# Head scales by transposes of a broadcast column, filling products kept for the end of attention, and four stores moved to ScalarE, in a two-layer hybrid encoder

## The chip, the cores and the metric

The kernel runs on one core of one Trainium2 chip. The metric is device time in microseconds (us) of one launch, which does all of the work from the input arrays in device memory (DRAM) to the two outputs. TensorE does the matrix products and transposes, VectorE, ScalarE and GpSimd the elementwise work, and DMA queues, issued mostly by SyncE, move data between DRAM and the on-chip memories: SBUF, and PSUM, which has eight banks of 128 x 512 float32 and receives the results of TensorE. In the rows of the profile these engines are PE (PEld for its weight loads), DVE, ACT, POOL and SP.

## The reference

Two layers are applied to two sequences with the same weights: a prompt of 2048 rows and a sample of 512 rows, each row 1024 wide.

```python
def layer(x, l, ...):
    h = rms_norm(x, pre_g)
    proj = h @ w_in                                    # 1024 -> 3072
    u, zp, q, k, v, za = split(proj)                   # 512 each
    pool_out = multiscale_pool(u, pool_w, pool_scale) * silu(zp)
    q, k = rope(q), rope(k)                            # 4 heads, 2 maps, 64 wide
    o = diff_attention(q, k, v, lam)                   # softmax(q1 k1) v - lam * softmax(q2 k2) v
    o = rms_norm(o, subln_g, 1e-5) * (1 - lambda_init) # over the 128 of each head
    attn_out = o * silu(za)
    y = concat(pool_out, attn_out) @ w_out             # 1024 -> 1024
    return x + rms_norm(y, post_g)
```

Everything is float32. Attention is bidirectional (no mask), each sequence attends to itself only, and its four heads have values of 128 columns.

## The kernel before, in words

**Number format.** [...] The kernel splits an operand into a high and a low half (`split`: a copy to `F32R`, then a subtraction) and adds the products high x high, low x high and high x low, so one tile of 128 x 128 weights against 512 columns costs three products.

**Order of a layer** (`Layer.run`).

1. *Norm and projections.* Rows are normalised, transposed by TensorE and split (`hth`, `htl`), 512 rows at a time. `project` makes 128 x 512 blocks of `proj` in the four PSUM banks named `sc`, each with 24 products. `evacuate` takes such a block out of PSUM and stores it to DRAM: q and k with their rotation (`qs`, `ks`), v (`vs`), the pool inputs (`us`, `zs`), and the gate za as `(tanh(za/2) + 1) * za` in `gs`, one store for each of four heads and each 512 rows. All these stores are issued on SyncE.

2. *Attention* (`attention`). One block is 256 queries of one head; the prompt's last head alternates with the sample's blocks. The work runs in steps. A step of the steady state issues, in this order: four pairs of score products (`score`, L439 and L440, q high and q low against 512 keys) mixed with the four exponentials of the previous step's scores (`expo`, L466) and the maxima of this step (`peak`); one flip after the first pair and one after the last (`flip`, L491: four transposes of the exponentials into a `tr` bank, of which there are two; `split` then makes `ath` on ScalarE and `atl` on VectorE); the values products of the earlier step's late flip; the combination of the two softmax maps on GpSimd (`combine`, L481 and L482); filling products; and the values products of the early flip. `values` (L508) accumulates a block's output in the one PSUM bank `ot`. A prompt block takes four steps, and its values take eight flips.

When a block's last values are out, `finish` (L512 to L526) runs as a generator over the step: ScalarE copies `ot` to `oc`; between the early and the late flip's split VectorE makes `mt` = oc times a column `sg` times the gate `g`, which goes to DRAM (`mh`); after the late split ScalarE squares `oc` and copies the high half, and VectorE subtracts for the low half (`shl`). One step later `squares` multiplies these with a matrix of ones (L532), and `scales` takes from it the head's RMS scale for each query, `rstat`, 128 queries on the partitions and one column per head.

At the end of attention some steps have no scores: only flips, values and what is left of the finishing remain. I call them end steps.

3. *Filling products* (`fill`, called at L653). While attention runs, `fill(n)` issues up to n products of other work into the one PSUM bank `mm`: first the sample's projections to q, k, v and za (16 groups of 24 products, of which the first four steps take two groups, L277; for v, L249, `fill` counts two products of half the columns as one), then, after the second half of the weights `w_out` is loaded and split (steps without products), the pooled half of the output projection (`pooled_outputs`, 20 tiles of two groups of 12 products, L697), whose results go to DRAM (`ys`). Each group ends by yielding its evacuation, and there the loop of `fill` breaks, so that a call never passes the end of a group. n is 14 in steps 0 to 3 (`FIRST`) and 6 from then on (`FILL`). The evacuation begins in the next step. What is left after attention is issued in a row by a loop in `Layer.run`, which in this kernel finds nothing.

4. *Phase 3* (`phase3`). For each of 20 tiles of 128 rows (16 of the prompt, 4 of the sample), `load` fetches the pooled half `y` and `mixh` (the `mt` of four heads), and prepares `diag` on GpSimd: `rstat`'s four columns are split into a high and a low half (`r2`) and multiplied into identity matrices (L764). `scale` multiplies ones with the eight diagonals, two products into a `tr` bank (L771), so that each head's scale stands on every partition, 128 queries along the columns. VectorE multiplies the bank with `mixh` to `mixs`, and splits it to `hl`: the high half is copied on ScalarE, the low half subtracted on VectorE. `products` issues 24 products (L784) into two `sc` banks, VectorE adds `y`; `post` squares on ScalarE, scales on VectorE, adds the residual `xr` on GpSimd (L834) and stores. `scale` for tile n + 1 runs beside the products of tile n. In layer 0 the last tiles also carry the norm of the next layer's first rows (`prepare`).

**Who sets the order.** On TensorE, ScalarE, VectorE and GpSimd instructions run in the order in which the program issues them. On SyncE a planner places them; it issues in order, and a store whose data is late holds back those behind it. Buffers in SBUF come in pools with a fixed number of turns (`bufs`), and `reuse_waits="tile"` makes the next user of a buffer wait for the last reader.

Of the kernel before, what the change touches and what calls it, by code (L numbers as in the profile page):

```python
# [15 lines left out]
ALU = mybir.AluOpType  # L16
# [25 lines left out]
FIRST = 14  # L42
WGAP = 3
# [7 lines left out]
def f32(ap):  # L51
    return ap.bitcast(F32)
# [3 lines left out]
def trunk_kernel(ctx: ExitStack, tc: tile.TileContext, a, outs):  # L56
# [227 lines left out]
    def evacuate(st, sl, kind, pair, sub, ps, cs, raws, p):  # L284
# [7 lines left out]
        if kind in ("za", "zp"):  # L292
            th = p["t"].tile([P, TB], F32, name="rb")
            nc.scalar.activation(th, ps, AF.Tanh, scale=0.5)
            o = p["t"].tile([P, TB], F32, name="ra")
            nc.scalar.activation(o, ps, AF.Copy)
            yield
            nc.vector.scalar_tensor_tensor(o, th, 1.0, o, op0=ALU.add, op1=ALU.mult)
            nc.sync.dma_start(st["gs" if kind == "za" else "zs"][h][:, sl], o)
            return  # L300
# [92 lines left out]
    def attention(c, p, po, fill):  # L393
# [118 lines left out]
        def finish(b):  # L512
            st, h, qb, ot = b["st"], b["h"], b["qb"], b["ot"]
            qs = slice(qb * QB, (qb + 1) * QB)
            oc = p["o"].tile([P, QB], F32, name="oc")
            nc.scalar.activation(oc, ot[:, :QB], AF.Copy)  # L516
            yield
            mt = p["o"].tile([P, QB], F32, name="mt")
            nc.vector.scalar_tensor_tensor(mt, oc, c["sg"], b["g"], op0=ALU.mult, op1=ALU.mult)
            nc.sync.dma_start(st["mh"][:, h, qs], mt)  # L520
            yield
            shl = p["o"].tile([P, 2, QB], F32R, name="shl", bufs=2)
            nc.scalar.activation(oc, oc, AF.Square)
            nc.scalar.activation(shl[:, 0], oc, AF.Copy)
            nc.vector.tensor_tensor(shl[:, 1], oc, f32(shl[:, 0]), op=ALU.subtract)  # L525
            closing.append((b, oc, shl))  # L526
# [63 lines left out]
        while True:  # L590
# [62 lines left out]
            fill(FILL if step > 3 else FIRST)  # L653
# [84 lines left out]
    def phase3(l, wo, scaling, pairs, kept, es, nxt):  # L738
# [4 lines left out]
        m_p = mixed.enter_context(sbuf("m", 2))  # L743
# [5 lines left out]
        def load(st, t):  # L749

            s = dict(st=st, t=t, y=y_p.tile([P, D], F32, name="y"))
            nc.sync.dma_start(s["y"], st["ys"][t * P : (t + 1) * P, :])
            t0 = t // 2 * 2 * P
            key = st["n"], t0
            if key not in pairs:
                pairs[key] = d_p.tile([P, H, 2 * P], F32, name="mixh")
                nc.sync.dma_start(pairs[key], st["mh"][:, :, t0 : t0 + 2 * P])
            s["h"] = pairs[key][:, :, t % 2 * P : (t % 2 + 1) * P]
            r = st["rstat"][:, t, :]
            r2 = small.tile([P, 2, H], F32R, name="r2")  # L760
            split(r2[:, 0], r2[:, 1], r, nc.gpsimd, nc.gpsimd)
            s["diag"] = d_p.tile([P, 2 * H, P], F32R, name="diag")
            wide = f32(r2).rearrange("p i h -> p (i h)").unsqueeze(2).to_broadcast([P, 2 * H, P])
            nc.gpsimd.tensor_tensor(s["diag"], ident.unsqueeze(1).to_broadcast([P, 2 * H, P]), wide, op=ALU.mult)  # L764
            tiles.append(s)

        def scale(s):

            ps = bank("tr")
            for i in range(2):  # L770
                nc.tensor.matmul(ps, lhsT=ones, rhs=s["diag"][:, i * H : (i + 1) * H, :].rearrange("p h n -> p (h n)"), start=i == 0, stop=i == 1)  # L771
# [4 lines left out]
            split(s["hl"][:, 0], s["hl"][:, 1], m, nc.scalar, nc.vector)  # L776
# [66 lines left out]
        for _ in scale(tiles[0]):  # L843
            pass
        scaling = []
        for n in range(len(order)):
# [5 lines left out]
            if n + 1 < len(order):  # L852
                scaling.append(scale(tiles[n + 1]))
# [316 lines left out]
```

## Time and profile before

| | before |
|---|---|
| median of 3 runs | 3190.98 us (3190.53 to 3191.36) |
| profiled execution | 3190.91 us |
| its span, first to last instruction | 3189.1 us |
| TensorE busy (PE) | 3086.4 us, 97% |
| VectorE (DVE) | 2187.3 us, 69% |
| GpSimd (POOL) | 1859.2 us, 58% |
| ScalarE (ACT) | 1749.7 us, 55% |
| mean granted TensorE clock | 0.992 |
| DMA | 464.54 MB, mean 146 GB/s |

The times in the traces are counted from the span's start. A row of a group of instructions names its line, engine and operation, the tiles it writes and reads, the shape and the count, then the busy time and the mean duration of one, then the idle time in front and what ended it. A row of the timeline has the start, the duration, the engine, and the line, with the wait before it in square brackets. A row of a window has its bounds and length, then the busy time of PE, PEld, DVE, ACT and POOL with the number of their instructions (of PE and PEld alone where one line was asked for), then the granted clock, the busy share of the DMA engines and GB/s.

Attention runs from 630.89 to 1432.20 in layer 0 and from 2217.54 to 3015.93 in layer 1, each time up to the first end step. Phase 3 of layer 1 begins at 3045.21.

### The profile page before, as it was taken

To read this page: it belongs to the slowest core of one execution; us is meant where nothing else is said; L and a number is where in the kernel's file an instruction comes from. 1 tells how busy PE (TensorE), PEld (TensorE's weight loads), DVE (VectorE), ACT (ScalarE), POOL (GpSimd) and SP (SyncE) were. 2 spreads that over 40 slices of the span, in tenths; PEclk is the share of its full clock that TensorE was granted. 3 is DMA by queue.
4 is the path that set the end of the run, shared out by engine and by line. 5 is a ranking of instruction groups with operands and counts; after the bars stand their busy time and mean duration, and the time that the engine had idled before them with its cause. 6 is when DMAs were issued, how large, how long until landed. Compare 5 with 4: busy or idle time off the path is not lost. (4 is left out here: it accounts for less than half of the span.)

```text
span 3189.1 us, 48499 instructions
## 1 busy us (share of the span) xinstructions
PE 3086.4 (97%) x16936; PEld 2590.8 (81%) x16936; DVE 2187.3 (69%) x3289; ACT 1749.7 (55%) x3995; POOL 1859.2 (58%) x2058
## 2 busy tenths in 40 slices
PE   8999999999998999998899999999999999999988
PEld 6898888778887888887688888887788878888866
DVE  3354255678898887777834543555888988877777
ACT  3244233377777777772333432333787778777622
POOL 1000122289997988888810001222999979888888
PEclk9999999999999999999999999999999999999999
DMA  5354457643424334437754544577434253353367
GB/s 203 113 160 144 129 160 208 196 132 96 130 67 129 107 109 138 120 99 242 269 176 123 160 131 142 164 204 213 115 90 123 63 141 111 95 156 110 107 213 239
DMA packets 298901, 464.54 MB, mean 146 GB/s; under 512 B 26144, under 2 KB 180768, under 8 KB 298656
## 3 DMA queue, kind: packets, MB, share of 16 engines
q1 hardware_dynamic: 298656, 461.44, 48.4%
q8 instruction: 133, 2.18, 0.3%
q14 instruction: 112, 0.92, 0.1%
HBM read 293.57 MB, written 167.77 MB: 145 GB/s over the span
## 5 line engine op out<-in xcount | busy, mean ns | idle before, releaser
L466 ACT ACTIVATE e<-sc,nm 128x512 f32<-128x512 f32 x1088 | 733.3, 694 | 49.2 <-DVE nm L453 39.7
L450 DVE TENSOR_REDUCE mx<-sc 128x1 f32<-128x512 f32 x1024 | 648.1, 682 | 143.5 <-PE sc L440 141.9
L482 POOL TENSOR_TENSOR e<-e,e 128x1024 f32<-128x1024 f32 (+1 forms) x288 | 666.4, 2314 | 24.0
L277 PE MATMUL sc<-hth,wh 128*128 128x512 f32 x1408 | 555.4, 394 | 0.1
L277 PE MATMUL sc<-htl,wh 128*128 128x512 f32 x1408 | 554.1, 394 | 0.2 <-DVE htl L114 0.2
L277 PE MATMUL sc<-hth,wl 128*128 128x512 f32 x1408 | 552.4, 392 | 0.0
L439 PE MATMUL sc<-ks,q 128*128 128x512 f32 x1024 | 435.6, 425 | 11.8 <-DMA ks<-ks_p 5.3
L109 ACT ACTIVATE ath<-tr 128x512 fp32r<-128x512 f32 x544 | 327.9, 606 | 215.6 <-PE ot L508 167.6
L440 PE MATMUL sc<-ks,q 128*128 128x512 f32 x1024 | 405.5, 396 | 0.0
L114 DVE TENSOR_TENSOR atl<-tr,ath 128x512 fp32r<-128x512 f32 x544 | 364.0, 682 | 43.5 <-ACT ath L109 43.5
L508 PE MATMUL ot<-ath,v 128*128 128x256 f32 x2176 | 369.3, 292 | 3.1 <-ACT oc L516 1.9
L491 PE MATMUL tr<-ident,e 128*128 128x128 f32 x2176 | 330.6, 275 | 18.0 <-DVE atl L114 17.3
L167 POOL TENSOR_TENSOR rs<-ss,mhalf 128x1 f32<-128x1 f32 x40 | 27.1, 676 | 550.2 <-DVE ss L165 550.2
L491 PEld LDWEIGHTS tr<-ident,e 128*128 128x128 f32 x2176 | 267.3, 141 | 98.1 <-DVE atl L114 30.8
L481 POOL TENSOR_SCALAR e<-e,nco 128x1024 f32<-128x1024 f32 (+1 forms) x288 | 337.9, 1173 | 15.0
L508 PEld LDWEIGHTS ot<-ath,v 128*128 128x128 f32 x2176 | 312.1, 190 | 23.7 <-ACT oc L516 2.7
L277 PEld LDWEIGHTS sc<-hth,wl 128*128 128x128 f32 x1408 | 264.5, 188 | 59.3 <-POOL wl L114 0.2
L277 PEld LDWEIGHTS sc<-hth,wh 128*128 128x128 f32 x1408 | 264.5, 188 | 58.4 <-issue 0.3
L277 PEld LDWEIGHTS sc<-htl,wh 128*128 128x128 f32 x1408 | 264.5, 188 | 57.6 <-DVE htl L114 0.5
L439 PEld LDWEIGHTS sc<-ks,q 128*128 128x128 f32 x1024 | 193.9, 189 | 79.7 <-ACT e L466 47.6
L114 DVE TENSOR_TENSOR wl<-wr,wh 128x1024 fp32r<-128x1024 f32 x94 | 121.7, 1298 | 180.9 <-ACT wh L109 178.8
L466 ACT ACTIVATION_READ_ACCUMULATOR e<-sc,nm 128x1 f32 x1088 | 231.0, 212 | 0.0
(149 smaller groups left out, 5978.0 us busy)
## 6 DMA issues: line engine op xcount, KB each, us to landing
wr<-in_w_in SPq DMA_DIRECT2D x128, 512.0 KB, 4.2
q<-qs_p SPq DMA_DIRECT2D x128, 256.0 KB, 4.1
ks_p<-hl SPq DMA_DIRECT2D x64, 256.0 KB, 3.4
vs_p<-hl SPq DMA_DIRECT2D x128, 128.0 KB, 2.7
qs_p<-hl SPq DMA_DIRECT2D x64, 256.0 KB, 3.5
mp_p<-hl SPq DMA_DIRECT2D x32, 512.0 KB, 3.7
ks<-ks_p SPq DMA_DIRECT2D x64, 256.0 KB, 5.7
v<-vs_p SPq DMA_DIRECT2D x32, 512.0 KB, 5.9
```

Source lines behind the costliest of these rows:

```text
L109: nc.scalar.activation(hi, src, AF.Copy)
L114: lo_eng.tensor_tensor(lo, src, f32(hi), op=ALU.subtract)
L167: nc.gpsimd.tensor_tensor(rs, ss, mhalf[:, :1], op=ALU.pow)
L277: nc.tensor.matmul(ps, lhsT=w[k // 4][m][:, k % 4, ns], rhs=h[:, k, :], start=k + i == 0, stop=k == KT - 1 and i == 2)
L439: nc.tensor.matmul(ps, lhsT=q[:, m, 0, ts], rhs=kk, start=True, stop=False)
L440: nc.tensor.matmul(ps, lhsT=q[:, m, 1, ts], rhs=kk, start=False, stop=True)
L450: nc.vector.reduce_max(s["mx"][:, ch : ch + 1], s["ps"][ch], axis=AX.X)
L466: nc.scalar.activation(dst, s["ps"][ch], AF.Exp, bias=s["nm"], accum_out=s["b"]["z"][s["qt"]][:, m, ch : ch + 1])
L481: nc.gpsimd.tensor_scalar(x1[:, :n], x1[:, :n], nco, 0.0, op0=ALU.mult, op1=ALU.add)
L482: nc.gpsimd.tensor_tensor(x0[:, :n], x0[:, :n], x1[:, :n], op=ALU.add)
L491: nc.tensor.transpose(ps[:, j, qt * P : (qt + 1) * P], e[kt // 8][:, kt % 8 * P : (kt % 8 + 1) * P], ident)
L508: nc.tensor.matmul(b["ot"][:, :QB], lhsT=b["vs"][v][kt // 8][:, kt % 8, :], rhs=at[:, j, :], start=unit + i == 0, stop=kt == nkt - 1 and i ...
```

## The change

- `finish` has no copy `oc`. ScalarE squares `ot` itself to `sq`, VectorE makes `mt` from `ot` in PSUM, and the split of the square is one call of `split`, at the same place in the step as before.
- `fill` is called with 5 in every third step and with 6 in the others after the first four; in steps without new scores it is called with 10 (`LAST`). The first four still have 14.
- In phase 3 there are no `r2` and `diag`. `scale` transposes, for each head, the column of `rstat` broadcast over 128 columns, so four transposes stand in place of two products. The low half of `hl` is made on GpSimd in place of VectorE. The pool `m` has three turns in place of two, and `scale` runs two tiles ahead in place of one.
- In `evacuate`, the stores of the gate za for the prompt's heads 2 and 3 and its rows from 1024 on (four stores in a layer) are issued by ScalarE in place of SyncE.

```diff
+LAST = 10
...
             nc.vector.scalar_tensor_tensor(o, th, 1.0, o, op0=ALU.add, op1=ALU.mult)
-            nc.sync.dma_start(st["gs" if kind == "za" else "zs"][h][:, sl], o)
+            last = kind == "za" and pair == 1 and st is pr and sl.start >= 2 * TB
+            (nc.scalar if last else nc.sync).dma_start(st["gs" if kind == "za" else "zs"][h][:, sl], o)
...
         def finish(b):
             st, h, qb, ot = b["st"], b["h"], b["qb"], b["ot"]
             qs = slice(qb * QB, (qb + 1) * QB)
-            oc = p["o"].tile([P, QB], F32, name="oc")
-            nc.scalar.activation(oc, ot[:, :QB], AF.Copy)
-            yield
+            sq = p["o"].tile([P, QB], F32, name="sq")
+            nc.scalar.activation(sq, ot[:, :QB], AF.Square)
             mt = p["o"].tile([P, QB], F32, name="mt")
-            nc.vector.scalar_tensor_tensor(mt, oc, c["sg"], b["g"], op0=ALU.mult, op1=ALU.mult)
+            nc.vector.scalar_tensor_tensor(mt, ot[:, :QB], c["sg"], b["g"], op0=ALU.mult, op1=ALU.mult)
             nc.sync.dma_start(st["mh"][:, h, qs], mt)
             yield
+            yield
             shl = p["o"].tile([P, 2, QB], F32R, name="shl", bufs=2)
-            nc.scalar.activation(oc, oc, AF.Square)
-            nc.scalar.activation(shl[:, 0], oc, AF.Copy)
-            nc.vector.tensor_tensor(shl[:, 1], oc, f32(shl[:, 0]), op=ALU.subtract)
-            closing.append((b, oc, shl))
+            split(shl[:, 0], shl[:, 1], sq, nc.scalar, nc.vector)
+            closing.append((b, sq, shl))
...
-            fill(FILL if step > 3 else FIRST)
+            fill(FIRST if step <= 3 else FILL - (step % 3 == 0) if nxt else LAST)
...
-        m_p = mixed.enter_context(sbuf("m", 2))
+        m_p = mixed.enter_context(sbuf("m", 3))
...
-            r = st["rstat"][:, t, :]
-            r2 = small.tile([P, 2, H], F32R, name="r2")
-            split(r2[:, 0], r2[:, 1], r, nc.gpsimd, nc.gpsimd)
-            s["diag"] = d_p.tile([P, 2 * H, P], F32R, name="diag")
-            wide = f32(r2).rearrange("p i h -> p (i h)").unsqueeze(2).to_broadcast([P, 2 * H, P])
-            nc.gpsimd.tensor_tensor(s["diag"], ident.unsqueeze(1).to_broadcast([P, 2 * H, P]), wide, op=ALU.mult)
...
             ps = bank("tr")
-            for i in range(2):
-                nc.tensor.matmul(ps, lhsT=ones, rhs=s["diag"][:, i * H : (i + 1) * H, :].rearrange("p h n -> p (h n)"), start=i == 0, stop=i == 1)
+            for h in range(H):
+                wide = s["st"]["rstat"][:, s["t"], h : h + 1].to_broadcast([P, P])
+                nc.tensor.transpose(ps[:, h * P : (h + 1) * P], wide, ident)
...
-            split(s["hl"][:, 0], s["hl"][:, 1], m, nc.scalar, nc.vector)
+            split(s["hl"][:, 0], s["hl"][:, 1], m, nc.scalar, nc.gpsimd)
...
-        for _ in scale(tiles[0]):
-            pass
         scaling = []
+        for s in tiles[:2]:
+            for _ in scale(s):
+                pass
...
-            if n + 1 < len(order):
-                scaling.append(scale(tiles[n + 1]))
+            if n + 2 < len(order):
+                scaling.append(scale(tiles[n + 2]))
```

## The prediction

> **What bounds the kernel now.** I read the page first (engine shares), then the core's busy time by stretch (windows), the chain, the timeline of single steps, and the groups by line.
>
> ```profile
> PE 3086.4 (97%) x16936; PEld 2590.8 (81%) x16936; DVE 2187.3 (69%) x3289; ACT 1749.7 (55%) x3995; POOL 1859.2 (58%) x2058
> ```
>
> TensorE is busy 97% of the span, the others 55 to 81%. So I look for the stretches in which TensorE is not dense. In attention it is dense: windows give busy us and (xinstructions) of PE, PEld, DVE, ACT, POOL, then the granted clock; the chain merges six filling products.
>
> ```profile
> 2613.77:2658.60 44.83, 44.83 (x279) 39.05 (x277) 37.40 (x65) 35.87 (x94) 38.57 (x45) 1.00 0.46 142
> ...
> 2264.35 1.39 PE mm L277 x6
> ```
>
> These are two blocks, eight steps: 5.60 us a step, PE 100%, POOL 86%, DVE 83%, ACT 80%. A filling product costs 1.39 / 6 = 0.232 us; without its six a step has 4.21 us of PE work.
>
> TensorE loses time in three places. Attention's end:
>
> ```profile
> 3017.80 0.39 PE L697 MATMUL mm<-wol,mixp 128*128 128x512 f32 x1
> ...
> 1432.20:1458.89 26.69, 19.77 (x125) 16.40 (x123) 16.85 (x28) 12.61 (x29) 23.27 (x40) 0.89 0.52 159
> 3015.93:3045.21 29.28, 20.30 (x125) 16.81 (x123) 19.27 (x28) 12.59 (x29) 20.53 (x30) 0.86 0.34 109
> 3045.21:3054.02 8.81, 8.81 (x26) 6.71 (x27) 2.75 (x4) 0.63 (x1) 8.09 (x17) 0.69 1.04 389
> ```
>
> The last filling product starts at 3017.80, and the stretch from the first step without scores (3015.93) to phase 3's first product lasts 29.28 us (26.69 in layer 0). Its own work is 66 values products of half the columns (0.12 us), ten flips of four transposes (0.4, below), six filling products and ten others: 7.9 + 4.0 + 1.4 + 1.0 = 14.3 us. So 15 and 12.4 us are lost; the first tile then takes 8.81 us instead of 6.06 at a granted clock of 0.69. Attention's start:
>
> ```profile
> 2214.41 1.72 SPq L418 DMA_DIRECT2D ks<-ks_p  x3
> 2219.57 0.33 SPq L299 DMA_DIRECT2D gs_p<-ra  x1
> ...
> 2221.07 5.75 DMA ks<-ks_p
> ...
> 630.89:656.96 26.07, 21.96 (x82) 16.67 (x80) 11.36 (x21) 12.77 (x32) 12.03 (x11) 0.87 0.80 226
> 2217.54:2240.05 22.51, 19.72 (x81) 14.28 (x79) 11.37 (x21) 12.66 (x32) 10.53 (x10) 1.00 0.88 260
> ```
>
> SyncE issues in order: of the key loads (ks) some go out at 2214.41, the next stand behind a gate store (gs) that waits for VectorE until 2219.57, and land 5.75 us after 2221.07. Four steps take 26.07 and 22.51 us. Phase 3 (the rows count its products, 24 to a tile):
>
> ```profile
> 1504.14:1545.82 41.68, 36.15 (x145) 26.53 (x144) 1.00 0.84 279
> 1545.82:1584.88 39.06, 27.43 (x97) 19.48 (x96) 0.91 0.74 249
> 3054.02:3084.32 30.30, 28.80 (x122) 22.50 (x120) 1.00 0.62 194
> 3090.86:3167.33 76.47, 66.23 (x266) 48.64 (x264) 1.00 0.79 255
> ...
> 3095.83 2.41 POOL L834 TENSOR_TENSOR y<-y,xr 128x1024 f32<-128x1024 f32 x1
> 3096.22 2.56 DVE L114 TENSOR_TENSOR hl<-mixs,hl 128x512 fp32r<-128x512 f32 x1 [1.19 <-ACT hl L109]
> 3098.84 0.50 PE L784 MATMUL sc<-woh,hl 128*128 128x512 f32 x1 [0.64 <-DVE hl L114]
> 3100.93 1.90 POOL L764 TENSOR_TENSOR diag<-ident,r 128x1024 fp32r<-128x1024 f32 x1
> ```
>
> In layer 1 the early tiles take 30.30 / 5 = 6.06 us, the eleven later ones 76.47 / 11 = 6.95. The low half (hl) runs 2.56 us on VectorE beside POOL's y addition, and TensorE waits for it. In layer 0 six tiles take 6.95, the next four 39.06 us.
>
> **The change, part by part.** The sum is made against the profiled execution, 3190.9 us (span 3189.1); the median of the runs, 3191.0, is the same.
>
> *Phase 3.* Per tile POOL loses the two splits of r and diag (1.90), and gets the low half; VectorE loses the low half.
>
> ```profile
> L114 POOL TENSOR_TENSOR wol<-wor,woh 128x512 fp32r<-128x512 f32 x16 | 21.5, 1342 | 16.2 <-ACT woh L109 16.2
> ...
> 1564.43 0.62 PE L771 MATMUL tr<-diag,ones 128*128 128x512 f32 x2
> 1564.89 0.60 PE L176 MATMUL tr<-ident,xt 128*128 128x128 f32 x4
> 1565.24 0.71 PE L784 MATMUL sc<-woh,hl 128*128 128x512 f32 x2
> ```
>
> The low half on POOL is bounded by 1.34 (same size) and 2.56 (what it takes on VectorE); I take 1.34, since the row is POOL's own. POOL then has 2.41 + 1.34 and two one-column operations in 6.06 us. In its queue the low half stands before those, and can delay a tile's y by that 1.34; only the store waits for y. The third m buffer and the buffers that diag leaves add no instruction. With hl ready two tiles ahead the 0.64 wait goes: 76.47 − 11 × 6.06 = 9.8 in layer 1, 41.68 − 6 × 6.06 = 5.3 in layer 0. Layer 0's four tiles lose 39.06 − 24.2 − 1.7 (16 transposes of the next layer's norm) = 13.1; the contending pair (diag, low half) is gone, but the norm's own waits stay: 0 to 13, I take 10. Two products cost 0.46 (1564.43 to 1564.89), four transposes 0.35, and 0.08 more on the next weight load: −0.03 x 40 = −1. How a stationary operand read from one broadcast column loads isn't shown: 0.35 to, with each at its recorded 0.6/4 and no overlap, 0.6; I take 0.43. **−26.**
>
> *The four stores per layer on ScalarE.* Eight issues leave SyncE; the loads behind them go out up to ten us sooner. On ScalarE each issue (0.33, as on SyncE) waits for the VectorE result; queued behind it are evacuations and, after the last, exponentials that need scores first, so no cost. Four steps of 14, 10, 14, 10 products hold 4 × 1.85 of scores (eight products) and 48 × 0.232 = 18.5; 4.6 at least per step (below) makes 19.5. Gain 6.6 + 3.0; bounds 0 and that. **−9.5.**
>
> *Filling.* A call of fill stops where a group ends. Now 24 products (projections) take four steps of 6, and 12 (pooled) two. With 5 in every third step groups no longer end on a step: 24 take five steps (6, 6, 5, 6, 1 or 5, 6, 6, 5, 2), 12 take three (5, 6, 1). Counting the loop: 139 steps follow the first four before the end steps; before the change they and the first end step issue all 14 × 24 + 40 × 12 = 816 products. After it 70 steps serve the 14 projection groups, four go to weights, 65 serve 21 pooled groups and 11 products; nine end steps issue 1 + 10 + 2 + 10 + 2 + 10 + 2 + 10 + 2 = 49. So 211 products (48.9 us) leave the 139 steps, 43 more run in the end steps, and 168 (14 groups, 38.9 us) run in a row after the loop. Product time is only moved; three things are not:
>
> (a) After the loop every group waits for the one mm bank.
>
> ```profile
> 2843.84 0.39 PE L697 MATMUL mm<-wol,mixp 128*128 128x512 f32 x1
> 2844.27 0.60 ACT L721 ACTIVATE yo<-mm 128x512 f32<-128x512 f32 x1 [0.99 <-PE mm L697]
> ```
>
> From the last product's start to ScalarE's end is 1.03, and a hand-over takes 0.04 (2844.23 to 2844.27). Less the normal spacing, 0.23, each group's successor starts 0.84 late: 28 × 0.84. Bounds: 0.6 (the 0.60 of the copy alone) and 1.1. **+24.**
>
> (b) A step of one product has 4.39 us of PE work, but how short can it be? The barest shown has no product:
>
> ```profile
> 2563.10 0.40 PE L439 MATMUL sc<-ks,q 128*128 128x512 f32 x1
> 2566.50 0.60 ACT L109 ACTIVATE ath<-tr 128x512 fp32r<-128x512 f32 x1 [0.80 <-PE ot L508]
> 2566.99 0.68 ACT L466 ACTIVATE e<-sc,nm 128x512 f32<-128x512 f32 x1
> 2567.97 0.39 PE L439 MATMUL sc<-ks,q 128*128 128x512 f32 x1
> ```
>
> Between the two score products (PE sc) the step took 4.87, with two products of ones (0.23) in it. Values that were left from the step before end at 2566.50; only then ath's second buffer is free, the exponentials follow at 2566.99, and the next step's first score needs the bank that the first of them reads: 2566.99 + 0.68 + 0.04 = 2567.71, 4.61 after the start. So a short step loses 4.61 − 4.39 = 0.22, or 0.25 with products of ones. Where a block finishes it loses more:
>
> ```profile
> 2410.48 0.40 PE L439 MATMUL sc<-ks,q 128*128 128x512 f32 x1
> 2414.04 0.68 DVE L114 TENSOR_TENSOR atl<-tr,ath 128x512 fp32r<-128x512 f32 x1
> 2414.12 0.39 ACT L516 ACTIVATE oc<-ot 128x256 f32<-128x256 f32 x1 [1.95 <-PE ot L508]
> 2414.88 0.69 ACT L466 ACTIVATE e<-sc,nm 128x512 f32<-128x512 f32 x1
> 2415.31 0.64 PE L508 MATMUL ot<-ath,v 128*128 128x256 f32 x4
> ...
> L519 DVE SCALAR_TENSOR_TENSOR mt<-oc,sg,g x80: 468/542/2018, 693.4 to 3039.5; 128x256 f32<-128x256 f32 x80
> ...
> L519 DVE SCALAR_TENSOR_TENSOR mt<-oc,sg,g 128x256 f32<-128x256 f32 x80 | 74.6, 933 | 0.0
> ```
>
> Now ot is free after oc. In the changed finish it is free when mt has read it on VectorE, and mt stands behind atl: 2414.72 + 0.47 = 2415.19. (mt's rows: 468 ns at least, 542 median, 933 mean; I take the least, since it reads PSUM then and waits less for POOL.) The next block's first values, at 2415.31, just fit after six products; after five they start 0.15 late, after one 1.1. A block has four steps, so a short one loses (3 × 0.24 + 1.1) / 4 = 0.45 in the mean; 14 + 22 of them in a layer, a few with two products, and some ten finishing steps of five make 17.5. Bounds per layer: 2 (PE ends them all) and 49 (no step shrinks). **+35.**
>
> (c) In the end steps 10 us of products meet 15 and 12.4 idle; those at flips delay flips, while the row of products keeps the clock up and hides the last scales: 5 to 14 per layer, 9 taken. After it the first tile waits 0.65 longer for POOL's low half, counted in. **−18.**
>
> *Stalls of the projection steps.*
>
> ```profile
> 2240.05:2563.10 323.05, 94.94 (x225) 42.35 (x225) 1.00 0.34 93
> ```
>
> 56 steps (x225: four score products each, and the next one's first) take 323 us, nine more than 56 x 5.60. Groups end on the same quarter of a block each time, where finish's VectorE work lies; with five steps they drift. 0 to 9 per layer, 5 taken. **−10.**
>
> *finish* gives back one ScalarE copy and the wait of oc's square on mt: nothing, under the PE of 100% in the two blocks above, and in short steps it is in (b).
>
> Sum: 24 + 35 − 18 − 9.5 − 26 − 10 = −4.5: 3186.
>
> **The rivals.**
> 1. Short steps shrink with PE. For: ScalarE is 80% and VectorE 83% busy, so they have slack. Against: the step at 2563.10 with no product took 4.87 and not 4.4. At 0.1 per short step, and 0.15 where five products finish a block, (b) is 10: 3161.
> 2. ot's release: if mt takes its present mean, 0.93 (second row), it ends at 2415.65, and values in each finishing step of the 64 long blocks start 0.40 late even after six products: +26, 3214, so slower. It decides from 0.53 on. For: mt still reads g from SBUF beside POOL. Against: its median is 0.54 even now. The Trainium skill, GPSIMD Engine Reference, section Key points, says that POOL shares its SBUF interfaces with VectorE instructions that have two SBUF inputs; with one of mt's moved to PSUM it would speak against this rival. The trace agrees so far as mt, with two, reaches 2.02; a run with one isn't shown.
> 3. Transposes of a broadcast column don't overlap, and each takes its recorded mean:
>
> ```profile
> L491 PE MATMUL tr<-ident,e 128*128 128x128 f32 x2176 | 330.6, 275 | 18.0 <-DVE atl L114 17.3
> ```
>
> 4 × 0.275 − 0.46 = 0.64 more in 40 tiles: +25, 3213. Against: four take 0.35 at 1564.89. The Trainium skill, TensorE: Matmul & The Clock Gate, Part 4: PE-mode transpose, has about 275 ns in a kernel and says that transposes don't count as PE activity for the clock; by it phase 3 would slow as in this rival. The granted clock of 1.00 in steps with eight transposes does not agree.
>
> **How the numbers follow.** Forecast 0.45, its own range 3176 to 3198 (phase 3 ±4, end ±5, stalls ±8); rival 1 0.27, rival 2 0.24, rival 3 0.04. A difference under 0.2% (6.4 us) can't be told from none. Of the forecast 0.17 lies under 3184.6, 0.25 within, 0.03 above 3197.4: faster 0.27 + 0.17, same 0.25, slower 0.03 + 0.28. The range takes in rivals 1 and 2: 3157 to 3216, leaving out about 1 in 10 on each side.
>
> **What would show it.** Phase 3 tiles at 6.0 to 6.1 us, no diag, no wait on hl. First four steps under 20 us, ks issued without a gs between. Filling products 5, 6, 1; fourteen pooled groups in a row after the loop, 3.6 us each; short steps 4.6 to 4.9, and 5.5 where a block finishes. Wrong if the row after the loop is short, if short steps reach 4.4, or if six-product finishing steps pass 5.6.

## The result: slower by 1.4%, and where the time went

The changed kernel takes 3239.1 us (median of 4 runs, 3231.67 to 3239.58) against 3191.17 before: a ratio of 1.0142, interval 1.0124 to 1.0159. Forecast was 3186, with 3157 to 3216 as the range. The profiled execution took 3239.58 us, its span is 3237.8. One execution of each of two runs below, 3772.08 and 3424.68 us with a granted clock of 0.75 and 0.87 where the others have 0.99, is left out of their medians.

The page of the changed kernel, two rows that answer to those of before (TensorE's share, and the values products, whose last columns are the idle time in front of them and what ended it):

```profile
PE 3106.2 (96%) x17016; PEld 2591.3 (80%) x17016; DVE 2059.5 (64%) x3249; ACT 1719.1 (53%) x3915; POOL 1769.3 (55%) x1978
...
L510 PE MATMUL ot<-ath,v 128*128 128x256 f32 x2176 | 372.4, 293 | 27.5 <-DVE mt L520 27.2
```

Every other engine has less to do than before, and TensorE waits 27.2 us for `mt` on VectorE; in the kernel before it waited 1.9 us for the copy `oc` in this place. The span by stage says more. Windows of before, then of the changed kernel; in each the 135 steps of attention from the first to the start of the last scored step, the end (from there to phase 3's first product), and phase 3 (in layer 0 to the next layer's first product):

```profile
630.89:1426.69 795.80, 776.96 (x4696) 659.75 (x4694) 666.49 (x1117) 601.54 (x1543) 687.63 (x763) 0.99 0.40 114
1426.69:1458.89 32.20, 25.28 (x159) 21.21 (x157) 20.98 (x34) 16.58 (x39) 27.12 (x45) 0.91 0.46 140
1458.89:1604.36 145.47, 133.12 (x551) 103.10 (x551) 113.67 (x115) 43.06 (x75) 120.24 (x113) 0.96 0.78 266
2217.54:3010.40 792.86, 774.96 (x4696) 657.46 (x4694) 667.60 (x1117) 601.41 (x1543) 687.24 (x763) 1.00 0.40 114
3010.40:3045.21 34.81, 25.83 (x159) 21.64 (x157) 23.41 (x34) 16.59 (x39) 24.40 (x35) 0.88 0.30 99
3045.21:3189.10 143.89, 126.82 (x518) 97.84 (x518) 104.24 (x102) 33.53 (x61) 122.48 (x122) 0.96 0.74 241
```

```profile
633.66:1406.02 772.36, 741.23 (x4484) 621.38 (x4483) 646.46 (x1117) 577.08 (x1490) 680.07 (x763) 0.99 0.38 106
1406.02:1493.47 87.45, 74.64 (x375) 58.42 (x374) 19.31 (x34) 25.23 (x54) 20.43 (x36) 1.00 0.45 143
1493.47:1636.10 142.63, 128.90 (x584) 103.11 (x585) 75.23 (x94) 42.85 (x75) 90.98 (x81) 0.95 0.83 275
2247.19:3019.28 772.09, 741.41 (x4484) 621.66 (x4483) 645.13 (x1117) 577.05 (x1490) 680.04 (x763) 0.99 0.38 106
3019.28:3106.71 87.43, 74.64 (x375) 58.40 (x373) 19.35 (x34) 25.22 (x54) 20.43 (x36) 1.00 0.55 185
3106.71:3237.80 131.09, 120.34 (x552) 96.88 (x552) 66.48 (x81) 34.70 (x61) 86.84 (x80) 0.97 0.71 234
```

Attention is 23.4 and 20.8 us shorter, its end 55.3 and 52.6 longer, phase 3 2.8 and 12.8 shorter. The 211 products that left the steps of each layer are 211 x 0.232 = 49 us of TensorE's time. The end has them in full and some 5 us more. The steps, which should be 49 us shorter for them and 3 to 6 for the earlier stores, gave back less than half. Single steps of the changed kernel show how: a plain step with one product, a finishing step with one (a finishing step is one in which a block's last values come out), the step after a short one (here it finishes a block too), a step without flips near attention's end (I call it held) and one in the projections, which also finishes a block:

```profile
2753.29:2758.02 4.73, 4.65 (x32) 3.92 (x30) 4.39 (x9) 3.02 (x9) 4.56 (x4) 1.00 0.00 0
2736.69:2742.19 5.50, 4.65 (x32) 3.88 (x30) 4.33 (x8) 3.56 (x10) 4.90 (x11) 1.00 0.28 100
2758.02:2763.72 5.70, 5.70 (x35) 4.55 (x34) 4.71 (x9) 4.70 (x13) 5.18 (x11) 1.00 0.46 141
2906.92:2911.20 4.28, 3.38 (x17) 2.05 (x16) 3.58 (x6) 3.06 (x11) 4.20 (x3) 1.00 0.86 205
2345.26:2353.56 8.30, 4.92 (x32) 3.97 (x31) 7.94 (x11) 5.50 (x16) 7.70 (x12) 0.99 0.00 0
```

By their products they should take 4.39, 4.39, 5.32 (five products), 3.2 (the same step takes 4.36 with six, in a run below) and 4.39. The plain one loses 0.34, the finishing one 1.11, the step after a short one 0.38, and the held one hardly shrinks at all: 4.28 with one product, 4.36 with six. The last one is 3.9 us too long; the timeline of it follows below.

### The profile page after: what moved, and what is told of

Its sections match the earlier page's. It is cut to its first block, busy times and chain, and to the rows that moved or that the text cites. A ratio compares the mean times of both kernels' runs of the same rounds, so it can differ in the third digit from the quotient of the medians.

```text
span 3237.8 us, 48438 instructions
## 1 busy us (share of the span) xinstructions
PE 3106.2 (96%) x17016; PEld 2591.3 (80%) x17016; DVE 2059.5 (64%) x3249; ACT 1719.1 (53%) x3915; POOL 1769.3 (55%) x1978
## 5 line engine op out<-in xcount | busy, mean ns | idle before, releaser
L441 PE MATMUL sc<-ks,q 128*128 128x512 f32 x1024 | 444.5, 434 | 14.0 <-ACT e L468 13.9
L442 PE MATMUL sc<-ks,q 128*128 128x512 f32 x1024 | 407.2, 398 | 0.0
L510 PE MATMUL ot<-ath,v 128*128 128x256 f32 x2176 | 372.4, 293 | 27.5 <-DVE mt L520 27.2
L483 POOL TENSOR_SCALAR e<-e,nco 128x1024 f32<-128x1024 f32 (+1 forms) x288 | 321.2, 1115 | 14.9
L278 PEld LDWEIGHTS sc<-hth,wh 128*128 128x128 f32 x1408 | 264.9, 188 | 58.5 <-POOL wl L115 0.3
L510 PE MATMUL ot<-atl,v 128*128 128x256 f32 x1088 | 224.3, 288 | 8.0 <-DVE atl L115 6.3
```

The costliest lines, as they stand in the source:

```text
L278: nc.tensor.matmul(ps, lhsT=w[k // 4][m][:, k % 4, ns], rhs=h[:, k, :], start=k + i == 0, stop=k == KT - 1 and i == 2)
L441: nc.tensor.matmul(ps, lhsT=q[:, m, 0, ts], rhs=kk, start=True, stop=False)
L442: nc.tensor.matmul(ps, lhsT=q[:, m, 1, ts], rhs=kk, start=False, stop=True)
L483: nc.gpsimd.tensor_scalar(x1[:, :n], x1[:, :n], nco, 0.0, op0=ALU.mult, op1=ALU.add)
L510: nc.tensor.matmul(b["ot"][:, :QB], lhsT=b["vs"][v][kt // 8][:, kt % 8, :], rhs=at[:, j, :], start=unit + i == 0, stop=kt == nkt - 1 and i ...
```

## The experiments

Two theories stood at the start. *Filling*: the loss is in the steps that don't shrink and the row of products after attention. *Finish*: the output bank `ot`, now released by `mt` on VectorE, holds TensorE up whatever the filling. The first three runs undo one or both; times are medians, with the ratio to the kernel before.

**The filling of before**

```diff
-            fill(FIRST if step <= 3 else FILL - (step % 3 == 0) if nxt else LAST)
+            fill(FILL if step > 3 else FIRST)
```

> The changed kernel with the filling of before (6 products a step, none kept). Theory 'filling' (the loss is the uneven groups of 5, 6, 1 products, whose short steps don't shrink, and the row of products after attention): attention's steps are back at 5.55 us, the first four at 20.1, phase 3 keeps its gain of 12.8 and 4.9 us, and the time is 3191 - 8.5 - 17.7 = 3165 us. Rival 'finish' (the output bank, now released by mt on VectorE, holds TensorE up whatever the filling): steps in which a block finishes stay above 5.6 us, TensorE waits on mt for 20 us or more, and the time is 3180 to 3215.

Measured: 3143.38 us, ratio 0.9851 (0.9835 to 0.9867), better than either theory had it. Windows of this run (layer 0's phase 3, then attention and end of layer 1, whose phase 3 takes 133.3 us):

```profile
1448.92:1582.40 133.48, 128.49 (x584) 103.76 (x585) 77.02 (x94) 43.88 (x75) 91.25 (x82) 0.95 0.84 289
2194.29:2981.85 787.56, 772.35 (x4695) 657.83 (x4694) 647.43 (x1117) 587.85 (x1507) 681.78 (x763) 1.00 0.40 114
2981.85:3010.78 28.93, 23.86 (x164) 20.15 (x162) 18.75 (x34) 14.95 (x36) 20.07 (x36) 1.00 0.34 103
```

So the filling costs 3239 - 3143 = 96 us. Of 49 us of products, attention in layer 1 gives back 787.56 - 772.09 = 15.5, and the end grows by 58.5. Finishing steps with six products take 5.55, so the finish holds up nothing there; the rival falls.

**The finish of before**

```diff
-            nc.scalar.activation(sq, ot[:, :QB], AF.Square)
+            nc.scalar.activation(oc, ot[:, :QB], AF.Copy)
+            yield
...
-            nc.vector.scalar_tensor_tensor(mt, ot[:, :QB], c["sg"], b["g"], op0=ALU.mult, op1=ALU.mult)
+            nc.vector.scalar_tensor_tensor(mt, oc, c["sg"], b["g"], op0=ALU.mult, op1=ALU.mult)
```

> The changed kernel with the finish of before (copy oc, mt from oc). Theory 'filling': only what TensorE waits on mt can come back (65 us of idle time of TensorE and of its weight loads together, which overlap, so 10 to 30 us); the finishing steps with one product shrink from 5.50 to some 4.8, the steps of one product elsewhere stay at 4.73, and the time is 3210 to 3229, slower than before. Rival 'finish': 3190 or less.

Measured: 3229.55 us, ratio 1.0127 (1.0112 to 1.0142), some 10 us below the changed kernel. Finishing steps of one product take 5.24 (some 4.8 was expected), so most of their floor isn't `mt`; but the long step above is gone: 5.23 in place of 8.30 at the same place, where the block now finishes a step later, in 5.86.

**Both of before** (only phase 3 and the stores changed; the two edits above together)

> Only phase 3 and the four stores are changed; filling and finish are those of before. Both theories: 3165 us (3191 less 8.5 in the first steps of attention and 17.7 in phase 3). What tells: if the new finish is harmless with six products a step, this equals the run with the filling of before and the new finish within 3 us; if the finish holds TensorE up, this one is 10 us or more below it.

Measured: 3158.53 us, ratio 0.9901 (0.9887 to 0.9916). It is 15 us above the run with the new finish, so with six products a step the new finish is a gain, not nothing. From the windows: the ends 32.14 and 32.17 us against 28.94 and 28.93, attention 791.61 and 789.84 against 787.63 and 787.56, layer 0's phase 3 136.77 against 133.48.

What holds the plain short step? The timeline of the changed kernel, from one step's first score product to the next one's:

```profile
2785.22 0.40 PE L441 MATMUL sc<-ks,q 128*128 128x512 f32 x1
...
2788.64 0.60 ACT L110 ACTIVATE ath<-tr 128x512 fp32r<-128x512 f32 x1 [0.98 <-PE ot L510]
2788.71 0.16 DVE L455 TENSOR_REDUCE nm<-mx 128x1 f32<-128x4 f32 x1
2789.14 0.68 ACT L468 ACTIVATE e<-sc,nm 128x512 f32<-128x512 f32 x1
2789.96 0.50 PE L441 MATMUL sc<-ks,q 128*128 128x512 f32 x1
```

It is the chain that the prediction read from before: ScalarE's `ath` waits until the values products have read its buffer, the exponentials stand behind it, and the next score needs the bank that the first of them reads. A third buffer takes that wait away:

**Three flip buffers**

```diff
-            pa = open_pools(left, "left", e0=8, v=4, at=2, o=2, q=2, k=5, e1=3, raw=1)
+            pa = open_pools(left, "left", e0=8, v=4, at=3, o=2, q=2, k=4, e1=3, raw=1)
```

> The changed kernel with three buffers for ath and atl in place of two (one buffer of keys is given up for the room, which can cost at the head changes). Theory (a short step is held because ath of the late flip waits until values have read the buffer of the early flip before it, and the exponentials stand behind that on ScalarE): a step of one product that is not a finishing one takes 4.4 to 4.6 us in place of 4.73. Rival (the score bank, released by the first exponential, or the transposes' own bank holds it): 4.73 as now. Finishing steps of one product, held by mt, stay near 5.5 for both.

One execution: 3223.82 us, so without an interval. The same step now:

```profile
2771.01 0.40 PE L441 MATMUL sc<-ks,q 128*128 128x512 f32 x1
...
2773.96 0.60 ACT L110 ACTIVATE ath<-tr 128x512 fp32r<-128x512 f32 x1 [0.51 <-PE tr L493]
2774.50 0.16 DVE L455 TENSOR_REDUCE nm<-mx 128x1 f32<-128x4 f32 x1
2774.75 0.69 ACT L468 ACTIVATE e<-sc,nm 128x512 f32<-128x512 f32 x1 [0.20 <-POOL e L484]
2775.65 0.43 PE L441 MATMUL sc<-ks,q 128*128 128x512 f32 x1
```

`ath` starts 2.95 us after the step's start in place of 3.42, but the step is only 0.1 shorter, 4.64: the first exponential now waits 0.20 us for GpSimd's addition (named in the bracket), and the maximum `nm` on VectorE ends at 2774.66, no earlier. The theory had the wait right and its worth wrong; other plain short steps stay at 4.72. Behind one floor lies the next. Attention is 4.8 and 5.2 us shorter than in the changed kernel; part of that lies in the steps behind a short one, 5.47 in place of 5.58.

**Four products in every step**

```diff
-            fill(FIRST if step <= 3 else FILL - (step % 3 == 0) if nxt else LAST)
+            fill(FIRST if step <= 3 else 4 if nxt else LAST)
```

> The changed kernel with 4 products in every step from the fifth on (10 in end steps, as there): 12 products take three steps and 24 take six, so the mean per step is about that of the changed kernel (12 in 5, 6, 1), but even. If the unevenness is what costs: 22 steps of layer 1 from its 79th on take 22 x 5.09 + 10 x 0.116 + some 2 for five finishing steps = 115 us in place of the 120.1 of the changed kernel, and a plain step takes 5.1; the time is 3225 to 3233. If short steps are held by a floor that does not depend on evenness (ScalarE's exponentials and the banks), a step of four takes 5.3 or more, and the time is 3239 or more.

Measured: 3242.22 us, ratio 1.0164 (1.0149 to 1.0179), above the 3225 to 3233 of the theory and within what the rival had. Two steps of it, plain and finishing:

```profile
2766.15:2771.25 5.10, 5.10 (x35) 4.38 (x33) 4.19 (x7) 4.65 (x13) 5.02 (x3) 1.00 0.94 225
2781.64:2787.15 5.51, 5.36 (x35) 4.39 (x33) 4.33 (x8) 4.43 (x13) 5.08 (x10) 1.00 0.45 143
```

A plain step of four is dense, as expected. But a finishing step takes 5.51, as with one product (5.50), so each of the 32 long blocks of a layer loses 0.3 to 0.4, and there are more products left for the end, which takes 107 us. Evenness heals the plain steps and nothing else. GpSimd is busy 5.02 of 5.10 us in that plain step, but this does not make it the next floor: plain steps of one product take 4.73.

**`mt` ahead of the early flip's low half**

```diff
-            if early:
-                flip_split(early[2])
...
+            for g in finishing:
+                next(g)
+            if early:
+                flip_split(early[2])
```

> The changed kernel with mt issued on VectorE ahead of the early flip's low half (atl), in place of behind it. Theory (a finishing step with few products takes 5.50 because ot is released by mt, which stands behind atl): mt ends 0.6 us earlier, the new block's first values start then, and the finishing steps of one product take some 5.2 in place of 5.50, those of five 5.33 in place of 5.50; over 64 blocks that is 5 to 15 us, so 3224 to 3234. Rival (the floor of these steps is VectorE's whole queue, maxima, atl and mt together, in whatever order): 5.5 stays, 3239.

Measured: 3245.59 us, ratio 1.0186 (1.0165 to 1.0206): the theory fell. The finishing step of one product takes 5.72. Its turn of the bank, against the same turn in the changed kernel:

```profile
2736.73 0.40 PE L510 MATMUL ot<-atl,v 128*128 128x256 f32 x2
2737.16 0.38 ACT L518 ACTIVATE sq<-ot 128x256 f32<-128x256 f32 x1 [2.51 <-PE ot L510]
2737.58 0.48 DVE L520 SCALAR_TENSOR_TENSOR mt<-ot,sg,g 128x256 f32<-128x256 f32 x1 [0.42 <-ACT sq L518]
2738.21 0.71 PE L510 MATMUL ot<-ath,v 128*128 128x256 f32 x4 [0.85 <-DVE mt L520]
```

```profile
2739.90 0.40 PE L510 MATMUL ot<-atl,v 128*128 128x256 f32 x2
2740.33 0.38 ACT L518 ACTIVATE sq<-ot 128x256 f32<-128x256 f32 x1 [1.94 <-PE ot L510]
2740.85 0.47 DVE L520 SCALAR_TENSOR_TENSOR mt<-ot,sg,g 128x256 f32<-128x256 f32 x1
2741.38 0.73 PE L510 MATMUL ot<-ath,v 128*128 128x256 f32 x4 [0.85 <-DVE mt L520]
```

Both turns take 1.08 us from the last old product's end to the first new one. `mt` does not start before `sq` has ended, though it writes nothing that `sq` reads: what the two share is the bank that both read. In this run VectorE stands idle until `sq` has ended ahead of 76 of the 80 `mt`, 43.4 us in all. So `atl` in front of `mt` had cost 0.1 at most, and the new order put `sq` ahead of `ath` and so delayed the flips and, 0.5 us later in the step than before, the exponentials. That the finish of before gave 5.24 fits: there `oc` alone releases the bank, and its turn takes 0.48. The Trainium skill, PSUM — Partial Sum Buffer, section PSUM bank collisions raise a hardware error, says that two engines must be kept from one bank at the same time, reads against reads included; the start of `mt` 0.04 us after the end of `sq` agrees.

The long step of the projections, changed kernel:

```profile
2344.11 2.75 POOL L484 TENSOR_TENSOR e<-e,e 128x1024 f32<-128x1024 f32 x1
2344.52 2.89 DVE L314 TENSOR_TENSOR t<-ra,cs 128x512 f32<-128x512 f32 x1
2352.70 0.74 PE L510 MATMUL ot<-ath,v 128*128 128x256 f32 x4 [3.03 <-DVE mt L520]
```

A rotation product of k takes 2.89 us on VectorE beside GpSimd's addition, where its usual time is 0.68, and all that is queued behind it, `mt` (at 2352.17) last, is late. The forecast had let this collision get rarer with groups of five steps; it got worse at two places a layer (the other, with the rotation of q, takes 8.67), since now it holds a bank.

**The row on four banks**

```diff
-                ps = bank("mm")
+                ps = bank("sc" if idle[0] else "mm")     # idle[0] is set just ahead of the row
```

> The changed kernel, whose row of 168 products after attention takes the four score banks, idle by then, in place of the one mm bank. Theory (the row loses 0.97 us a group to the wait for the bank: 53.15 us for 170 products that need 39.4): the row takes 39 to 41 us in each layer, the end from the last scored step to phase 3 goes from 87.4 to some 74, and the time from 3239 to 3212, still slower than before. Rival (the mix loads or ScalarE's copies set the row's pace, 3.8 us a group): the row stays at 50 or more and the time at 3235 or more.

Measured: 3217.83 us, ratio 1.0088 (1.0073 to 1.0103), 21 us below the changed kernel. In the changed kernel the row is

```profile
1438.28:1491.43 53.15, 42.89 (x170) 30.63 (x170) 1.00 0.52 164
```

170 products, 39.4 us of work, 13.7 lost to the bank. With four banks the ends go from 87.45 and 87.43 to 74.87 and 79.80; in layer 1 three loads of `mixp` come late instead (0.95, 1.81 and 1.32 us of waiting).

**Six products a step, 48 kept**: the idea alone, without uneven steps and without a row

```diff
-            fill(FIRST if step <= 3 else FILL - (step % 3 == 0) if nxt else LAST)
+            fill(FIRST if step <= 3 else FILL if nxt else LAST, nxt)
...
+                if on and po and kept_back[0] <= 0:     # 480 - 48, counted down
+                    return
```

> The changed kernel with 6 products in every step as before, but the last 48 (four groups) kept for the end steps, so no uneven steps and no row after the loop: the idea of keeping products by itself. Against the run with the filling of before (3143 us; its last eight scored steps have 6 products each and its end takes 28.9 us). Theory (a step does not get shorter than some 4.7 us, a finishing one than 5.5, and the end absorbs at most half of what is kept): the last eight steps give back 4 to 5 us a layer in place of 11.1, the end takes 5 to 6 us more, so 3142 to 3147: nothing gained. Rival (the end has 12 to 15 us of idle time that products fill for nothing): 3130 to 3136.

Measured: 3161.26 us, ratio 0.991 (0.9894 to 0.9927), 18 us above the run with nothing kept. The end takes 35.71 and 35.69 in place of 28.94 and 28.93, attention gives back 4.0 and 2.5 us, where 4 to 5 were expected, and layer 0's phase 3 takes 144.6 in place of 133.5, which I had not expected. The time so misses the expected 3142 to 3147, but not towards the rival: 36 of the 48 products, 8.4 us, leave the 135 steps of a layer, the steps give back less than half of it, and the end takes 6.8 us more. Nothing is gained by keeping products.

**The stores on SyncE again**, from the run with the filling of before

```diff
-            (nc.scalar if last else nc.sync).dma_start(st["gs" if kind == "za" else "zs"][h][:, sl], o)
+            nc.sync.dma_start(st["gs" if kind == "za" else "zs"][h][:, sl], o)
```

> The run with the filling of before (3143 us), with the four gate stores back on SyncE. Theory (the loads of keys stood behind these stores): the first four steps take 26.1 and 22.5 us again in place of 20.1, the rest is equal, 3150 to 3153. Rival (the earlier start came from elsewhere): first four steps 20.1, 3143.

Measured: 3153.21 us, ratio 0.9882 (0.9866 to 0.9899): 10 us for four stores a layer. The first four steps with the stores on SyncE, in both layers, which together are as long as expected:

```profile
632.21:655.62 23.41, 20.73 (x82) 15.75 (x80) 11.36 (x21) 12.68 (x32) 11.28 (x10) 0.93 0.85 252
2197.67:2222.75 25.08, 20.73 (x81) 15.77 (x80) 11.36 (x21) 12.67 (x32) 10.92 (x10) 0.93 0.85 234
```

They take 20.95 and 20.83 in the run with the filling of before, and 20.06 and 20.05 in the changed kernel.

**Phase 3 by parts**, from the run with the filling of before: one tile ahead; the low half on VectorE; all of phase 3 as before (its edit is shown in part)

```diff
-        for s in tiles[:2]:
+        for s in tiles[:1]:
...
-            if n + 2 < len(order):
-                scaling.append(scale(tiles[n + 2]))
+            if n + 1 < len(order):
+                scaling.append(scale(tiles[n + 1]))
```

> The run with the filling of before (3143 us), with scale running one tile ahead in phase 3 in place of two; the low half stays on GpSimd and the transposes stay. Theory (the gain of phase 3 comes from the low half's leaving VectorE, whose 2.56 us became 1.3 to 1.7 on GpSimd): the tiles lose some, since the low half stands behind an addition of 2.4 us on GpSimd: 6.1 to 6.9 us a tile, 3145 to 3160. Rival (one tile ahead is enough now): 6.03 a tile, 3143.

Measured: 3144.69 us, ratio 0.9857 (0.9842 to 0.9872), 6.03 us a tile. The rival holds.

```diff
-            split(s["hl"][:, 0], s["hl"][:, 1], m, nc.scalar, nc.gpsimd)
+            split(s["hl"][:, 0], s["hl"][:, 1], m, nc.scalar, nc.vector)
```

> The run with the filling of before (3143 us), with the low half of hl back on VectorE; transposes and two tiles ahead stay. Theory (the tiles of 6.95 us before came from VectorE's low half contending with GpSimd's work and being needed at once; one tile ahead is enough, as the last run showed, because the pair on GpSimd is gone): either half of the change is enough, so layer 1 keeps 6.03 to 6.1 us a tile, since with two tiles ahead nobody waits for the low half; layer 0's late tiles, whose wait is VectorE's queue, get longer by 0.7 to 2.6 us each: 3143 to 3155. Rival (VectorE's busy time itself is what limits): 6.3 to 6.9 us a tile, 3150 to 3168.

Measured: 3141.77 us, ratio 0.9859 (0.9836 to 0.9883), 6.03 us a tile; of layer 0's late tiles one took 14.5 us in place of 13.3, the others the same. The low half in phase 3 of layer 1, grouped with its mean duration in ns, in the kernel before; then one low half of this run, also on VectorE, and the addition of `y` on GpSimd that follows it:

```profile
L114 DVE TENSOR_TENSOR hl<-mixs,hl 128x512 fp32r<-128x512 f32 x20 | 38.8, 1939 | 23.0 <-ACT hl L109 22.3 <-DMA xr<-xs_p 0.7
```

```profile
3086.19 0.69 DVE L115 TENSOR_TENSOR hl<-mixs,hl 128x512 fp32r<-128x512 f32 x1 [0.74 <-ACT hl L110]
3088.82 2.39 POOL L829 TENSOR_TENSOR y<-y,xr 128x1024 f32<-128x1024 f32 x1 [2.27 <-DVE y L827]
```

The same instruction takes 0.69 us in the mean in place of 1.94, on the same engine. `diag` is not what had slowed it: before, in layer 1, 14 of the 20 low halves took 2.08 to 2.56 us, each of them beside the addition of `y` and none beside `diag`. That addition is still there; the low half is now made ahead of it. How much of this shift in time is due to the missing `diag`, and how much to the second tile ahead, no run separates. So neither the move of the low half nor the second tile ahead is needed for the gain, each taken by itself (both together weren't tried); that `diag` went is what the two runs share, and no run keeps it with the rest changed.

```diff
+            s["diag"] = d_p.tile([P, 2 * H, P], F32R, name="diag")
...
+            for i in range(2):
+                nc.tensor.matmul(ps, lhsT=ones, rhs=s["diag"][...], start=i == 0, stop=i == 1)
-                nc.tensor.transpose(ps[:, h * P : (h + 1) * P], wide, ident)
...
-            split(s["hl"][:, 0], s["hl"][:, 1], m, nc.scalar, nc.gpsimd)
+            split(s["hl"][:, 0], s["hl"][:, 1], m, nc.scalar, nc.vector)
```

> The run with the filling of before (3143 us), with phase 3 as before (diag on GpSimd, two products, low half on VectorE, one tile ahead). Theory: phase 3 returns to 145.5 and 143.9 us from 133.5 and 133.3, so 3143 + 22 = 3165 us. Rival (part of phase 3's gain is the new finish, whose last scales come earlier): 3155 to 3160.

Measured: 3166.78 us, ratio 0.993 (0.9914 to 0.9947); phase 3 takes 145.8 and 144.9 us. The theory holds: phase 3 as a whole is worth 23 us.

## Why the prediction was wrong

By terms, over both layers, from the spans (3237.8 - 3189.1 = 48.7):

| term | forecast | measured | from |
|---|---|---|---|
| (a) row after the loop, bank waits | +24 | +27 | 2 x (53.15 - 39.4) |
| (b) short steps | +35 | +67 | 2 x 49 leave attention, 15.3 and 15.5 come back (changed against filling of before) |
| (c) attention's end | -18 | -8 | 2 x 58.5 - 2 x 49 - 27 |
| stores | -9.5 | -8.5 | 26.07 and 22.51 to 20.06 and 20.05 |
| phase 3 | -26 | -16 | -2.8 and -12.8 |
| stalls of the projection steps | -10 | 0 | collisions, in (b) |
| finish | 0 | -14 | run with the filling of before: attention -5 beside the stores, ends -3.3 and -5.9 |
| elsewhere | 0 | +1 | +2.8 ahead of attention, -2.1 in layer 1's projections |

**The step that failed is (b)**, the price of a short step, with its mechanism right and its size half. The plain short step was forecast to lose 0.24 and loses 0.25 to 0.34; the finishing step of one product 1.1, and measures 1.11; the finishing step of five 0.15, and measures 0.2. Left out were three kinds. The step behind a plain short one loses 0.1 to 0.3, and 0.4 where it finishes a block: what was late in the short step is late at the start of the next, and I had asked that only of the finishing ones. Twice a layer the new finish met a rotation, of k and of q. And the six held steps near attention's end hardly shrink; I had counted them as plain, with 0.24, and they lose 1.08 each (4.28 with one product, 4.36 with six). What holds such a step in the changed kernel is a chain over three engines:

```profile
2907.59 2.50 DVE L452 TENSOR_REDUCE mx<-sc 128x1 f32<-128x512 f32 x4 [0.96 <-PE sc L442]
2910.12 0.16 DVE L455 TENSOR_REDUCE nm<-mx 128x1 f32<-128x4 f32 x1
2910.38 0.68 ACT L468 ACTIVATE e<-sc,nm 128x512 f32<-128x512 f32 x1
2911.20 0.50 PE L441 MATMUL sc<-ks,q 128*128 128x512 f32 x1 [0.91 <-ACT e L468]
```

The next step's first score waits 0.91 us for the first exponential, which needs `nm`, which needs all four maxima on VectorE, and the scores for these had waited for the exponentials of the step before. GpSimd is busy for 4.20 of the 4.28 us, but no row of the step waits for it. The run with the finish of before agrees: there `mt` stands ahead of the four maxima, takes 1.81 us beside GpSimd's addition, and the same step takes 4.88.

In layer 1 the steps from the 79th on lose 18 us more than with the filling of before, where 22 x 0.45 = 10 was forecast; the steps of the projections and weights 16, where 6 was.

**(c) failed too**, though the sum for the end came out: against the kernel before, the two ends together are 17.6 us shorter than the products kept and (a) would make them, and 18 was forecast. That is luck. With nothing kept, in the run with the filling of before, the ends are already 3.3 and 5.9 us shorter, so the kept products filled 4 us of idle time a layer, not 9; forecasting the finish at nothing hid this. How much of the rest is flips that the products delay, no run isolates.

**The finish** was not nothing. "Under the PE of 100% in the two blocks" was true there, but the ends and the stalled steps are not dense. The held steps show one way: with `oc` and six products `mt` takes 1.55 us ahead of the maxima and the step 4.63, with the new finish 4.36. Whether the ends gain by the copy less on ScalarE or by the quicker `mt`, no run separates. These 14 us hid part of the miss in (b).

**Phase 3** was right in its number where it was read from rows (layer 1: 12.8; 6.03 us a tile), with the wrong pair named: the prediction calls `diag` and the low half contending, but its own rows have the low half (3096.22) beside the addition of `y` (3095.83), with `diag` 2 us behind it. The second tile ahead, by which it took the wait on `hl` away, was not needed. It was short in layer 0. There the four late tiles were forecast to get 10 of 13 us back, and the 16th became longer:

```profile
1593.37 1.06 ACT L165 ACTIVATE junk<-xt 128x1024 bf16<-128x1024 f32 x1 [6.05 <-DMA xt<-xs_p]
1594.55 0.15 DVE L166 TENSOR_SCALAR ss<-ss 128x1 f32<-128x1 f32 x1 [5.39 <-ACT junk L165]
1596.43 0.68 DVE L769 TENSOR_TENSOR mixs<-tr,mixh 128x512 f32<-128x512 f32 x1
1597.17 1.12 PE L177 MATMUL tr<-ident,xt 128*128 128x128 f32 x4 [7.86 <-DVE mixs L769]
```

The next layer's norm waits for its rows (`xt`), VectorE waits in order with it, and `mixs` of this layer stands behind. That was not the contending pair, and it stayed. The 16th tile takes 22.5 us here, 20 to 23 in every run with kept products, and 11 to 16 in the runs without; in layer 1, which has no next norm, all are alike. The SyncE rows of two of these runs have the loads of `xt` and `mixh` in different orders, but no run isolates that: why keeping products lengthens this tile stays open.

**The rivals.** Rival 1 (short steps shrink with TensorE) is excluded by 4.73 and 5.50. Rival 2 (`mt` slow, so `ot` released late even after six products) did not come (its 26 on top of the forecast make 3212, not 3214): the duration in ns of `mt`, minimum, median and maximum, was 468, 542 and 2018, and is now

```profile
L520 DVE SCALAR_TENSOR_TENSOR mt<-ot,sg,g x80: 470/476/485, 689.5 to 3048.2; 128x256 f32<-128x256 f32 x80
```

The Trainium skill's rule on the interfaces that GpSimd shares (GPSIMD Engine Reference, Key points) had spoken against this rival, and the row agrees: with one of its inputs in PSUM `mt` no longer slows beside GpSimd; with `oc` again, in the run with the finish of before, it reaches 2630. The slower time came by none of the rivals. Rival 3 did not come: the four transposes stand 0.35 to 0.36 us before the next product, though each is recorded with 0.27, and the granted clock over eleven tiles with them is 1.00.

Of what would show it: phase 3's tiles, the first four steps, the pattern 5, 6, 1 and the row came as written, with 3.8 us a group in place of 3.6. The sentence "short steps 4.6 to 4.9, and 5.5 where a block finishes" was right; the sum made from it was not, as it took these as the only losses.

The best version found is the changed kernel with the filling of before: 3143 us, 1.5% faster than the kernel before; with the low half on VectorE, or one tile ahead, it is the same within the noise (3142 and 3145). Of it phase 3 is worth 23, the finish 15 and the stores 10 us, each by its own run.

## What to carry to other kernels

Work taken out of a software-pipelined step comes back only down to the longest chain through the step's buffers and engines, even where each engine has slack; before moving filler, read the barest step of every kind (plain, finishing, held, and the one after it), and count the filler as moved, not saved. A step's cover is also its slack: the six products hid a bank turn of 1.08 us that showed at once under five. When an engine slows beside another, find out which instruction of the other runs at that moment, row by row, before naming the pair; here it was enough that the two no longer met, with both still there.

## What the runs showed of the hardware that was not expected

`sq` on ScalarE and `mt` on VectorE, both only reading the bank `ot`, ran one after the other (0.38 and 0.47 us, 0.04 between them where nothing else stood in front), and the bank's turn took 1.08 us, against 0.48 with `oc` as its only reader.

A subtraction of 128x512 with both inputs in SBUF on VectorE took 2.46 to 2.56 us where it began 0.4 to 0.5 us into GpSimd's addition of `y`, and 0.69 where the two did not meet. Each of the 14 slow ones in layer 1 before ended 0.55 us after that addition, and so did the rotation product of 2.89 us after GpSimd's `e`. `mt` with `ot` in PSUM ran beside the same kind of addition in 0.47 to 0.49.
